# Trainium2 kernel of a hybrid SSD, attention and convolution block: the order of scan, gates and conformer tail, and the engine of the probability sums

## Chip, cores and metric

One core of one Trainium2 chip. The metric is the device time of one execution in microseconds, over several executions. The engines are TensorE (PE; its weight loads are PEld), VectorE (DVE), ScalarE (ACT) and GpSimd (POOL); SyncE (SP) issues all DMA transfers. All values are 32-bit floats.

## The reference, cut

Two layers over 1024 positions and a context of 256, width 1024. In each layer one projection gives ten parts, and three branches are joined again:

```python
z, xbc, dtr, q, k, v, ga, ua, ub, gc = split_cols(h @ w_in[i])
# SSD: silu of a depthwise convolution of 5 taps over xbc, then a scan both ways in chunks of 128
y_diag = einsum(C B^T, exp(cum_l - cum_s) masked, x dt)      # inside a chunk
y_off  = einsum(C, state that enters the chunk, exp(cum))
y = (y_f + y_b + d_skip * xs) * silu(z);  ssd = rmsnorm(y)
# attention: 12 heads over 4 key heads, 1280 keys
attn = attend(rope(rmsnorm(q)), [k, k_ctx], [v, v_ctx]) * silu(ga)
# conformer: convolution of 31 taps over ua * sigmoid(ub)
conv = (silu(layernorm(dwconv(u))) @ pw_w + pw_b) * silu(gc)
x = x + gate * (concat[ssd, attn, conv] @ w_out[i])
```

The context goes through the same blocks, in the last layer only as far as keys, values and states need it. SSD: 12 heads of 64, 2 groups, state 128, forward and backward.

## The kernel before, in words

All 1280 positions are ten tiles of 128 (in the second layer, the last, most work is for eight). Every projection matmul is three matmuls of rounded halves (`mm3`, L210: hh with wth, hl with wth, hh with wtl), in pieces of 512, 512 and 256 columns. A layer goes through these stages:

1. Norms and the k, v and q projections, position by position.
2. The feature-major blocks (`phase_b`, `block` L623). A block is two units of 128 features x 1280 positions; a unit is 72 matmuls. There are 17: nine of them alternate xbc (x, B and C of the SSD) with ub and ua of the conformer, then three blocks of z, two of gc, three of ga. What a unit of the first nine gives is convolved on DVE, xbc with 5 taps (xcv), u with 31 (cac, a chain of `scalar_tensor_tensor`). The unit of z, gc or ga is gated (`gate` L590) and stored to DRAM (gz_d, gc_d, ga_d).
3. `cm_tail` (L656), the rest of the conformer, stands beside the gc and ga blocks: transposes of cac, layernorm on DVE (statistics, a `pow` of one column on POOL, xn, lv), silu on ACT, the pointwise projection in groups of up to four tiles, gating by gc.
4. Attention (`attn` L904). A unit is two heads and two tiles of queries, 512 columns; 24 units see all keys, and in the first layer six more only the context's. `maxima` computes queries x keys and reduces over the keys' columns on DVE (a_sm), `scores` computes them again with the maxima subtracted through an extra row (q_b, k_b), ACT takes the exponential into a_p, `values` multiplies by vs. The denominators need a sum over the ten key tiles: a_p come in five pairs of 128 x 1024, of which four additions (a_ac, L974 and L978) make one; a last one of 512 (a_a, L981) feeds two matmuls. The list NG says, unit by unit, how many of these additions run on POOL; the others run on DVE.
5. `ssd` (L710), beside attention. For the nine backward states (chunk 9 to 1), then for the ten chunks in the order 8, 9, 0 to 7: POOL scales x (s_wx L732, s_xd L777) and decays the state (s_tm L735); cumulated decays are broadcast from DRAM to 128 partitions by DMA (s_cb, four of 384 KB a chunk), POOL subtracts a column (s_e L788), ACT takes relu and exp, POOL multiplies by C B^T (s_cm, L791). PE sums the output in 72 matmuls (s_e and s_xd, and s_yo through msk), DVE gates with z (s_yz), POOL scales and SP stores to ys_d. The term of the entering state is a matmul of hf or hb with s_cT, scaled on DVE (s_of L803) and added to s_yo on POOL (L806). The backward states stay in SBUF, one buffer each.
6. The output projection in two halves (`out_half` L1081), with the next layer's norms.

The order in which each engine runs its instructions is fixed when the program is built: a scheduler lays them on a modelled time line, where `at(t)` gives a piece of code its earliest time, and each engine then runs its own list strictly in sequence, waiting for data and for buffers. Constants such as SSD_PACE and TAIL are such times. Tiles come from pools with rings of buffers (`bufs`), so the next user of a ring waits for the last reader of the buffer. Pools are opened and closed as a stack, on the left or the right side of SBUF; a pool that is opened where another was waits for the closed one's last user.

## Time and profile before

| | |
|---|---|
| median of 3 runs | 2925.08 us (2920.04 to 2926.33) |
| profiled execution, its own time | 2926.13 us |
| its span | 2924.1 us, 41057 instructions |
| PE busy, mean granted clock | 2714.5 us (93%), 0.965 |
| DVE, POOL, ACT busy | 2175.7 (74%), 1165.6 (40%), 1062.2 (36%) |
| DMA | 314.44 MB, mean 108 GB/s |

PE's busy time is that of matmuls that overlap in its pipeline, so 93% is not 93% of its peak. The shares are means over stages with different limits; the prediction cuts the span into stages. A page of the profile names instructions by line, engine, operation, output and inputs; after a bar come busy time, mean ns of one, and the idle time of the engine ahead of them with what ended it.

### The profile page before, as it was taken

The numbers are of one execution on the slowest core, as the hardware profiler recorded it, in microseconds if no ns is written. First come the engines' busy times: TensorE is split into PE (matmuls) and PEld (weight loads), VectorE is DVE, ScalarE is ACT, GpSimd is POOL, SyncE is SP. The second block draws the span as 40 slices with busy tenths as digits, with TensorE's granted clock in tenths as the row PEclk, the third lists the DMA queues.
The fourth block names the chain that finished last, engine by engine and source line by source line (L and its number), as shares of the span: only waits on it lengthen the run. The fifth ranks groups of instructions, "written<-read, shape, count | busy, mean of one in ns | idle before, by whom it ended". The sixth has DMA issues, their size and how long they took to land. (4 is left out here: it accounts for less than half of the span.)

```text
span 2924.1 us, 41057 instructions
## 1 busy us (share of the span) xinstructions
PE 2714.5 (93%) x15708; PEld 2111.4 (72%) x15708; DVE 2175.7 (74%) x2987; ACT 1062.2 (36%) x1801; POOL 1165.6 (40%) x832
## 2 busy tenths in 40 slices
PE   5999998999998888999999999999998998999998
PEld 3888876888856655666787998877886665666676
DVE  4476899973299989797445587999835989898644
ACT  4212221222245454454335222222224454644432
POOL 2244122232168677571112352222323667675111
PEclk9999998999999989899999999999999999999999
...
GB/s 237 191 159 66 56 55 65 90 98 105 115 137 108 73 88 84 74 68 130 205 147 162 114 76 67 55 63 107 102 127 151 73 98 72 103 59 62 164 152 143
DMA packets 284035, 314.44 MB, mean 108 GB/s; under 512 B 27606, under 2 KB 219190, under 8 KB 282814
## 3 DMA queue, kind: packets, MB, share of 16 engines
...
q14 instruction: 74, 0.61, 0.1%
...
## 5 line engine op out<-in xcount | busy, mean ns | idle before, releaser
L193 PE MATMUL m<-hh,wth 128*128 128x512 f32 (+1 forms) x1440 | 533.7, 371 | 0.1
L193 PE MATMUL m<-hl,wth 128*128 128x512 f32 (+1 forms) x1440 | 532.2, 370 | 0.0
L193 PE MATMUL m<-hh,wtl 128*128 128x512 f32 (+1 forms) x1440 | 531.6, 369 | 0.0
L199 ACT ACTIVATE a_p<-m 128x512 f32<-128x512 f32 x492 | 285.5, 596 | 373.1 <-PE m L193 362.7
L208 DVE SCALAR_TENSOR_TENSOR cac<-up,cmw,cac 128x1295 f32<-128x1295 f32 (+1 forms) x240 | 383.2, 1617 | 1.9
L935 DVE TENSOR_REDUCE a_sm<-m 128x1 f32<-128x512 f32 (+1 forms) x600 | 331.0, 583 | 52.8 <-PE m L193 50.2
L359 POOL TENSOR_TENSOR wtl<-wr,wth 128x1024 fp32r<-128x1024 f32 x68 | 201.9, 2969 | 404.2 <-ACT wth L199 404.1
L193 PEld LDWEIGHTS m<-hh,wth 128*128 128x128 f32 x1440 | 273.0, 190 | 47.8 <-ACT th L199 0.5
L193 PEld LDWEIGHTS m<-hh,wtl 128*128 128x128 f32 x1440 | 272.5, 189 | 48.1
L193 PEld LDWEIGHTS m<-hl,wth 128*128 128x128 f32 x1440 | 272.7, 189 | 47.3
L193 PE MATMUL m<-q_a,k_a 128*128 128x512 f32 (+1 forms) x656 | 255.3, 399 | 23.1 <-ACT a_p L199 10.9
L193 PE MATMUL m<-k_a,q_a 128*128 128x512 f32 (+1 forms) x600 | 242.0, 440 | 24.9 <-DVE a_sm L935 19.3
L193 PE MATMUL t<-a_p,vs 128*64 128x256 f32 x1968 | 250.9, 397 | 0.9 <-ACT a_p L199 0.4
L193 PE MATMUL m<-woh,yl 128*128 128x512 f32 x576 | 227.7, 397 | 6.1 <-DVE yl L1101 5.9
L193 PE MATMUL m<-woh,yh 128*128 128x512 f32 x576 | 226.6, 396 | 5.2 <-ACT yh L199 5.2
L193 PE MATMUL m<-wol,yh 128*128 128x512 f32 x576 | 226.6, 395 | 0.8 <-DVE wol L1077 0.8
L193 PE MATMUL m<-q_b,k_b 65*128 65x512 f32 (+1 forms) x656 | 223.1, 350 | 0.0
L193 PEld LDWEIGHTS t<-a_p,vs 128*64 128x64 f32 x1968 | 138.7, 142 | 89.1 <-issue 17.2
L193 PEld LDWEIGHTS m<-q_a,k_a 128*128 128x128 f32 x656 | 129.3, 197 | 84.3 <-ACT a_p L199 23.4
L193 PEld LDWEIGHTS m<-k_a,q_a 128*128 128x128 f32 x600 | 117.0, 201 | 99.6 <-DVE a_sm L935 38.2
L199 ACT ACTIVATE wth<-wr 128x1024 fp32r<-128x1024 f32 (+1 forms) x84 | 89.3, 1063 | 255.6 <-DMA wr<-in_wfm 136.2
L193 PE MATMUL m<-wth,hh 128*128 128x256 f32 (+1 forms) x608 | 173.6, 288 | 1.3 <-ACT wth L199 0.8
...
## 6 DMA issues: line engine op xcount, KB each, us to landing
...
s_cb<-cum_d SPq DMA_DIRECT2D x72, 384.0 KB, 3.7
...
s_x<-xt_d SPq DMA_DIRECT2D x38, 384.0 KB, 3.2
yf<-ys_d SPq DMA_DIRECT2D x36, 384.0 KB, 3.9
yf<-ya_d SPq DMA_DIRECT2D x36, 384.0 KB, 4.2
...
```

The source lines that it names most:

```text
L193: P.matmul(o, l, r, start=start, stop=stop)
L199: S.activation(o, i, f, **k)
L208: V.scalar_tensor_tensor(o, i, s, i1, op0, op1)
L359: (e or G).tensor_tensor(lo[:, s], raw, hi[:, s].bitcast(F32), ALU.subtract)
L935: V.tensor_reduce(sm[:, 2 * x + t, j:j + 1], ps[:, 0:kn], axis=AX.X, op=ALU.max)
```

## The change

- The z blocks move in among the convolution blocks (the first twelve blocks are now x0 u0 x1 z0 u1 x2 u2 z1 x3 u3 x4 z2); two gc and three ga blocks follow.
- `ssd` is now called from `phase_b`, with its pool on the left stack, beside the last five blocks, with SSD_PACE 11.5. The attention's pools are opened after it is closed.
- In `ssd`, the broadcast lands in the s_e ring itself (four buffers, four tiles a chunk) and the s_cb ring is gone; for the backward direction the subtraction and relu become six activations of 128 columns with a bias on ACT; the multiplication by s_cm goes from POOL to DVE; backward states go through DRAM (hb_d) and a ring of two; s_tm shares a ring of two with s_of; PSUM tiles are spread over three pools.
- `cm_tail` moves beside attention, in groups of two tiles, 28 apart (TPACE); the convolved u goes through DRAM (cc_d, ct).
- NG = [4]: all four additions of 128 x 1024 run on POOL in every unit.

```diff
@@ -19,14 +19,15 @@
...
-TAIL = 40.0
-SSD_PACE = 25.0
+TAIL = 24.0
+TPACE = 28.0
+SSD_PACE = 11.5
...
-NG = [0, 1]
+NG = [4]
...
@@ -64,12 +65,12 @@
 
 
 TM_UNITS = [("k", 0), ("v", 0), ("q", 0), ("q", 1)]
-FM_UNITS = []
-for _j in range(5):
-    FM_UNITS.append((("xbc", 2 * _j), ("xbc", 2 * _j + 1)))
-    if _j < 4:
-        FM_UNITS.append((("ub", _j), ("ua", _j)))
-for _n, _c in (("z", 3), ("gc", 2), ("ga", 3)):
+_u = [[(("xbc", 2 * j), ("xbc", 2 * j + 1)) for j in range(5)], [(("ub", j), ("ua", j)) for j in range(4)],
+      [(("z", 2 * j), ("z", 2 * j + 1)) for j in range(3)]]
+FM_UNITS = [_u[k][j] for k, j in ((0, 0), (1, 0), (0, 1), (2, 0), (1, 1), (0, 2), (1, 2), (2, 1), (0, 3), (1, 3), (0, 4),
+                                  (2, 2))]
+NF = len(FM_UNITS)
+for _n, _c in (("gc", 2), ("ga", 3)):
     FM_UNITS += [((_n, 2 * j), (_n, 2 * j + 1)) for j in range(_c)]
 
 CO = {}
@@ -264,6 +265,8 @@
     ys_d = dr([6, 128, T], "ys_d")
     ya_d = dr([6, 128, T], "ya_d")
     yc_d = dr([4, 128, T], "yc_d")
+    hb_d = [dr([128, 768], f"hb_d{c}") for c in range(NT)]
+    cc_d = [dr([128, T], f"cc_d{j}") for j in range(4)]
...
@@ -553,6 +556,9 @@
             for k in range(1, 31):
                 at(t0 + k * pace)
                 stt(o[:, 0:NCM], u[:, k:k + NCM], cw[:, j, k:k + 1], o[:, 0:NCM], ALU.mult, ALU.add)
+            Y.dma_start(out=cc_d[j][:, 0:1024], in_=o[:, 0:1024])
+            if not last:
+                Y.dma_start(out=cc_d[j][:, 1024:1280], in_=o[:, 1039:1295])
 
...
@@ -642,69 +648,73 @@
                 if n == "xbc":
                     conv_x(j, tt)
 
-        for i in range(9):
+        for i in range(NF):
             block(i)
         s2.close()
 
 
+        g0 = b2 + NF * 26
         s3 = ExitStack()
-        tlp = pool(s3, f"tl{l}")
-        g0 = b2 + 9 * 26
-        for i in range(9, 14):
-            block(i)
-
-        def cm_tail(c0):
...
-        cm_tail(g0 + TAIL)
-        for i in range(14, 17):
+        sp = pool(s3, f"sp{l}")
+        ssd(l, sp, g0, sv)
+        for i in range(NF, len(FM_UNITS)):
             block(i)
         s3.close()
         st.close()
-        return g0 + 8 * 26, sv, st_r
+        return g0 + (len(FM_UNITS) - NF) * 26, st_r
+
+
+    def cm_tail(l, tlp, c0):
+        last = l == depth - 1
+        at(c0 - 10)
+        pwh, pwl = wblock(tlp, tlp, a["pww"][l], "pw", 1)
+        hc = mk(tlp, [128, 16], "hc")
+        ts(V, hc[:, 0:8], colc[l][:, CO["lng"][0]:CO["lng"][0] + 8], 0.5, ALU.mult)
+        groups = [(b, 2) for b in range(0, 8 if last else NT, 2)]
+        for tb, tn in groups:
+            uh = mk(tlp, [128, 4, 256], "uh", F32R)
+            ul = mk(tlp, [128, 4, 256], "ul", F32R)
+            for t in range(tb, tb + tn):
+                at(c0 + TPACE * t - 8)
+                ct = mk(tlp, [128, 4, 128], "ct", bufs=2)
+                for j in range(4):
+                    Y.dma_start(out=ct[:, j], in_=cc_d[j][:, 128 * t:128 * t + 128])
+                at(c0 + TPACE * t)
+                ps = mk(px, [128, 4, 128], "x")
+                for j in range(4):
+                    tr(ps[:, j, :], ct[:, j], idf)
+                bs = mk(tlp, [128, 12], "bs", bufs=2)
...
+                at(c0 + TPACE * t + 6)
+                ps2 = mk(px, [128, 4, 128], "x")
...
+            n = tn * 128
+            for f in range(4):
+                at(c0 + TPACE * (tb + tn - 1) + 14 + 3 * f)
+                gcs = mk(tlp, [128, 256], "gcs", bufs=2)
+                Y.dma_start(out=gcs[:, 0:n], in_=gc_d[f][:, tb * 128:tb * 128 + n])
+                ps = mk(px, [128, 512], "x")
...
+                Y.dma_start(out=yc_d[f][:, tb * 128:tb * 128 + n], in_=gcs[:, 0:n])
 
 
     def ssd(l, sp, c0, sv):
@@ -731,7 +741,7 @@
             wx = mk(sp, [128, 768], "s_wx", bufs=2)
             G.tensor_tensor(hv(wx), hv(xt), bc(wd[:, c, hs]), ALU.mult)
             if hin is not None:
-                tm = mk(sp, [128, 768], "s_tm", bufs=1)
+                tm = mk(sp, [128, 768], "s_of", bufs=2)
                 G.tensor_tensor(hv(tm), hv(hin), bc(et[:, c, hs]), ALU.mult)
             for g in range(2):
                 ps = mk(px, [128, 512], "x")
@@ -742,29 +752,35 @@
                 else:
                     V.tensor_copy(ho[:, s], ps[:, 0:384])
 
-        hb = {9: None}
+        hp = None
         t0 = c0 + 1
         for c in range(9, 0, -1):
             at(t0)
             t0 += 2
             xt, bt = load(c)
-            ho = mk(sp, [128, 768], f"hb{c - 1}")
-            state(c, 1, xt, bt, hb[c], ho)
-            hb[c - 1] = ho
+            ho = mk(sp, [128, 768], "hb", bufs=2)
+            state(c, 1, xt, bt, hp, ho)
+            if c <= 8 or not last:
+                Y.dma_start(out=hb_d[c - 1], in_=ho)
+            hp = ho
...
-                bT = mk(sp, [128, 2, 128], "s_bT", bufs=2)
+                bT = mk(sp, [128, 2, 128], "s_bT", bufs=1)
                 cT = mk(sp, [128, 2, 128], "s_cT", bufs=2)
                 tk = slice(128 * c, 128 * c + 128)
                 Y.dma_start(out=bT, in_=bT_d[:, :, tk].rearrange("g p t -> p g t"))
                 Y.dma_start(out=cT, in_=cT_d[:, :, tk].rearrange("g p t -> p g t"))
                 gz = mk(sp, [128, 6, 128], "s_gz", bufs=1)
                 Y.dma_start(out=gz, in_=gz_d[:, :, tk].rearrange("g p t -> p g t"))
-                ps = mk(px, [128, 512], "x")
+                hbc = None
+                if c != 9:
+                    hbc = mk(sp, [128, 768], "hb", bufs=2)
+                    Y.dma_start(out=hbc, in_=hb_d[c])
+                ps = mk(pt, [128, 512], "t")
                 for g in range(2):
                     mm(ps[:, 128 * g:128 * g + 128], bT[:, g, :], cT[:, g, :], True, True)
                 cm = mk(sp, [128, 2, 2, 128], "s_cm", bufs=1)
@@ -780,24 +796,27 @@
                 for g in range(2):
                     for d in range(2):
                         h0 = 12 * d + 6 * g
-                        cb = mk(sp, [128, 6, 128], "s_cb", bufs=2)
+                        e = mk(sp, [128, 6, 128], "s_e", bufs=4)
                         src = cum_d[24 * c + h0:24 * c + h0 + 6, :].rearrange("h t -> (h t)")
-                        Y.dma_start(out=cb.rearrange("p h t -> p (h t)"),
+                        Y.dma_start(out=e.rearrange("p h t -> p (h t)"),
                                     in_=src.unsqueeze(0).to_broadcast([128, 768]))
-                        e = mk(sp, [128, 6, 128], "s_e", bufs=4)
-                        G.tensor_tensor(e, cb, bc(cum[:, c, h0:h0 + 6], 6, 128), ALU.subtract)
-                        act(e, e, AF.Relu, scale=-1.0)
+                        if d:
+                            for j in range(6):
+                                act(e[:, j], e[:, j], AF.Relu, scale=-1.0, bias=cum[:, c, h0 + j:h0 + j + 1])
+                        else:
+                            G.tensor_tensor(e, e, bc(cum[:, c, h0:h0 + 6], 6, 128), ALU.subtract)
+                            act(e, e, AF.Relu, scale=-1.0)
                         act(e, e, AF.Exp, scale=-1.0)
-                        G.tensor_tensor(e, e, cm[:, d, g].unsqueeze(1).to_broadcast([128, 6, 128]), ALU.mult)
+                        V.tensor_tensor(e, e, cm[:, d, g].unsqueeze(1).to_broadcast([128, 6, 128]), ALU.mult)
                         E[d, g] = e
                 yo = mk(sp, [128, 768], "s_yo", bufs=1)
                 G.tensor_tensor(hv(yo), hv(xt), bc(rc(l, "d")), ALU.mult)
-                for d, hin in enumerate((hf, hb[c])):
+                for d, hin in enumerate((hf, hbc)):
                     if hin is None:
                         continue
-                    tm = mk(sp, [128, 768], "s_of", bufs=1)
+                    tm = mk(sp, [128, 768], "s_of", bufs=2)
                     for g in range(2):
-                        ps = mk(px, [128, 512], "x")
+                        ps = mk(pv_, [128, 512], "v")
                         mm(ps[:, 0:384], cT[:, g, :], hin[:, 384 * g:384 * g + 384], True, True)
...
@@ -1124,14 +1143,14 @@
         last = l == depth - 1
         st, sr, sw = ExitStack(), ExitStack(), ExitStack()
         pp = pool(st, f"pp{l}")
-        c0, sv, st_r = phase_b(l, nh, b0, pp)
+        c0, st_r = phase_b(l, nh, b0, pp)
         kp = pool(st, f"kp{l}")
         pre = attn_prep(l, kp, c0)
         st_r.close()
         nh[0].close()
         ap = pool(st, f"ap{l}")
-        sp = sr.enter_context(tc.tile_pool(name=f"sp{l}", bufs=1, side="right"))
-        ssd(l, sp, c0, sv)
+        tlp = sr.enter_context(tc.tile_pool(name=f"tl{l}", bufs=1, side="right"))
+        cm_tail(l, tlp, c0 + TAIL)
         sr.close()
```

What this does to the order of instructions is shown at three places. The first is PE in layer 0, where the gate matmuls end. Ahead of the change, from the middle of attention; m are scores (q_a, q_b against k_a, k_b) or keys' maxima (k_a first), and x one group of the SSD's output:

```order
L193 MATMUL m_8963<-q_a_8429,k_a_6708 128x512
L193 MATMUL m_8963<-q_b_8430,k_b_6709 128x512
L193 MATMUL m_8968<-k_a_8696,q_a_8759 128x512
L193 MATMUL m_8971<-k_a_8696,q_a_8759 128x512
L193 MATMUL m_8974<-q_a_8429,k_a_6708 128x512
L193 MATMUL m_8974<-q_b_8430,k_b_6709 128x512
L193 MATMUL x_7004<-msk_74,s_yo_6993 64x128 x2
L193 MATMUL x_7004<-s_e_6967,s_xd_966_6961 64x128 x2
L193 MATMUL x_7004<-s_e_6974,s_xd_967_6963 64x128 x2
```

Now, at the last gate matmul (m from wth, wtl and h), and on to the next chunk's output:

```order
L194 MATMUL m_7671<-hl_168,wth_7511 128x256
L194 MATMUL m_7671<-hh_167,wtl_7512 128x256
L194 MATMUL v_5649<-ones_78,s_s_772_5644 128x1
L194 MATMUL x_5663<-s_wx_5656,s_b_5541 128x384
L194 MATMUL v_5723<-hf_5655,s_cT_5671 128x384
L194 MATMUL x_5797<-s_wx_5793,s_b_5668 128x384
L194 MATMUL v_5726<-hf_5655,s_cT_5671 128x384
L194 MATMUL v_5731<-hb_5676,s_cT_5671 128x384
L194 MATMUL v_5734<-hb_5676,s_cT_5671 128x384
L194 MATMUL t_5739<-msk_74,s_yo_5720 64x128 x2
L194 MATMUL t_5739<-s_e_5688,s_xd_789_5684 64x128 x2
L194 MATMUL t_5739<-s_e_5694,s_xd_790_5686 64x128 x2
```

The output groups stood among the attention's matmuls; now PE's list has nothing but the scan between the last gate matmul and the next chunk's output, and so it goes on for eight chunks.

The second place is POOL in one chunk of the scan, layer 0. Before, from the norm's pow of one chunk to the last row ahead of the next chunk's subtractions (a_g and a_ac are the attention's):

```order
L833 TENSOR_TENSOR s_rs_7053<-s_rs_7053,neg_82 128x1
L794 TENSOR_TENSOR s_yo_7114<-s_x_7066,rowc_8_86 128x768
L1013 TENSOR_TENSOR a_g_8893<-a_g_8893,a_rc_9082 128x256
L732 TENSOR_TENSOR s_wx_7310<-s_x_7189,d_wd_1698 128x768
L735 TENSOR_TENSOR s_tm_7181<-hf_7057,d_et_1697 128x768
L1013 TENSOR_TENSOR a_g_9033<-a_g_9033,a_rc_9158 128x256
L974 TENSOR_TENSOR a_ac_1599_9107<-a_p_9114,a_p_9138 128x1024
L791 TENSOR_TENSOR s_e_7088<-s_e_7088,s_cm_7079 128x768
L791 TENSOR_TENSOR s_e_7102<-s_e_7102,s_cm_7079 128x768
L791 TENSOR_TENSOR s_e_7095<-s_e_7095,s_cm_7079 128x768
L791 TENSOR_TENSOR s_e_7109<-s_e_7109,s_cm_7079 128x768
L806 TENSOR_TENSOR s_yo_7114<-s_yo_7114,s_of_7116 128x768
```

Now, one chunk from its first subtraction on:

```order
L807 TENSOR_TENSOR s_e_5962<-s_e_5962,d_cum_1699 128x768
L793 TENSOR_TENSOR s_xd_857_5958<-s_x_5940,d_dt_1693 128x768
L793 TENSOR_TENSOR s_xd_858_5960<-s_x_5940,d_dt_1693 128x768
L846 TENSOR_TENSOR s_yo_5920<-s_yz_5875,colc_7_84 128x768
L745 TENSOR_TENSOR s_of_5932<-hf_5792,d_et_1711 128x768
L807 TENSOR_TENSOR s_e_5978<-s_e_5978,d_cum_1699 128x768
L852 TENSOR_TENSOR s_rs_5925<-s_rs_5925,neg_82 128x1
L813 TENSOR_TENSOR s_yo_5994<-s_x_5940,rowc_8_86 128x768
L742 TENSOR_TENSOR s_wx_6204<-s_x_6077,d_wd_1712 128x768
L825 TENSOR_TENSOR s_yo_5994<-s_yo_5994,s_of_5996 128x768
L825 TENSOR_TENSOR s_yo_5994<-s_yo_5994,s_of_6004 128x768
```

The multiplications by s_cm are gone from POOL, there are two subtractions instead of four, and the attention's instructions are gone from among them. The two additions of s_of come last, just ahead of the next chunk's first subtraction.

The third is DVE in attention, layer 0, around the sum of one unit's exponentials. Before:

```order
L935 TENSOR_REDUCE a_sm_9116<-m_9213 128x1
L974 TENSOR_TENSOR a_ac_1600_9108<-a_p_9176,a_p_9198 128x1024
L935 TENSOR_REDUCE a_sm_9116<-m_9223 128x1
L974 TENSOR_TENSOR a_ac_1600_9108<-a_ac_1600_9108,a_p_9221 128x1024
L937 TENSOR_REDUCE a_nm_9117<-a_sm_9116 128x4
L978 TENSOR_TENSOR a_ac_1600_9108<-a_ac_1599_9107,a_ac_1600_9108 128x1024
L935 TENSOR_REDUCE a_sm_9278<-m_9280 128x1
L981 TENSOR_TENSOR a_a_1634_9253<-a_ac_1600_9108 128x512
L935 TENSOR_REDUCE a_sm_9278<-m_9292 128x1
L820 TENSOR_TENSOR s_yz_7124<-x_7125,s_gz_7074 128x384
```

Now (bs, xn and lv are the conformer tail's):

```order
L687 BN_STATS bs_8281<-x_8276 128x6
L209 SCALAR_TENSOR_TENSOR lv_1276_8262<-lth_8261,lv_1276_8262 128x512
L954 TENSOR_REDUCE a_sm_9175<-m_9267 128x1
L688 BN_AGGR bs_8281<-bs_8281 128x2
L956 TENSOR_REDUCE a_nm_9176<-a_sm_9175 128x4
L206 TENSOR_SCALAR bs_8281<-bs_8281 128x1
L954 TENSOR_REDUCE a_sm_9315<-m_9317 128x1
L1000 TENSOR_TENSOR a_a_1565_9294<-a_ac_1530_9168 128x512
L206 TENSOR_SCALAR xn_8286<-x_8276,bs_8281 128x512
L954 TENSOR_REDUCE a_sm_9315<-m_9327 128x1
```

No a_ac is left on DVE; a_a reads what POOL has summed, and the tail's layernorm stands between the maxima, its xn behind a pow on POOL.

More of the change, by code (lines that the diff above doesn't have):

```diff
@@ L535, in phase_b @@
         b2 = b0 + 130
-        cmp_ = pool(st, f"cm{l}")
         s2 = ExitStack()
+        cmp_ = pool(s2, f"cm{l}")
         up_p = pool(s2, f"up{l}")
@@ L575, in conv_x @@
                 at(t0 + XLAG)
-                sg = mk(gp, [128, NT, 128], "xsg")
+                sg = mk(xp_p, [128, NT, 128], "xsg")
                 for ta in (0, 4, 8):
@@ L706, in phase_b @@
         st.close()
-        return g0 + 8 * 26, sv, st_r
+        return g0 + (len(FM_UNITS) - NF) * 26, st_r
[19 more added lines that the diff above has]
+                bs = mk(tlp, [128, 12], "bs", bufs=2)
+                V.bn_stats(bs[:, 0:6], ps.rearrange("p j t -> p (j t)"))
+                V.bn_aggr(bs[:, 6:8], bs[:, 0:6])
+                rs_pow(bs[:, 9:10], bs[:, 7:8], 1.0, bs[:, 8:9], 1)
+                xn = mk(tlp, [128, 512], "xn", bufs=1)
+                ts(V, xn, ps.rearrange("p j t -> p (j t)"), bs[:, 6:7], ALU.subtract, bs[:, 9:10], ALU.mult)
+                at(c0 + TPACE * t + 6)
+                ps2 = mk(px, [128, 4, 128], "x")
+                for j in range(4):
+                    tr(ps2[:, j, :], xn[:, 128 * j:128 * j + 128], idf)
+                th = mk(tlp, [128, 4, 128], "lth", bufs=1)
+                v2 = mk(tlp, [128, 4, 128], "lv2", bufs=1)
+                for j in range(4):
+                    g, b = hc[:, j:j + 1], hc[:, 4 + j:5 + j]
+                    ts(V, v2[:, j], ps2[:, j], g, ALU.mult, b, ALU.add)
+                act(th, v2, AF.Tanh)
+                stt(v2, th, 1.0, v2, ALU.add, ALU.mult)
+                o = (t - tb) * 128
+                act(uh[:, :, o:o + 128], v2, AF.Copy)
+                G.tensor_tensor(ul[:, :, o:o + 128], v2, uh[:, :, o:o + 128].bitcast(F32), ALU.subtract)
+            n = tn * 128
[4 more added lines that the diff above has]
+                ps = mk(px, [128, 512], "x")
+                pwx, ux = (pwh, pwl), (uh, ul)
+                mm3(ps[:, 0:n], lambda x, k: pwx[x][:, k, 128 * f:128 * f + 128],
+                    lambda x, k: ux[x][:, k, 0:n], 4)
+                stt(gcs[:, 0:n], ps[:, 0:n], cc(l, "pwb", f), gcs[:, 0:n], ALU.add, ALU.mult)
+                ts(V, gcs[:, 0:n], gcs[:, 0:n], 0.5, ALU.mult)
+                Y.dma_start(out=yc_d[f][:, tb * 128:tb * 128 + n], in_=gcs[:, 0:n])
@@ L808, in ssd @@
                 for g in range(2):
-                    ps = mk(px, [128, 512], "x")
+                    ps = mk(pt, [128, 512], "t")
                     for f3 in range(3):
@@ L821, in ssd @@
                                     gz[:, 3 * g:3 * g + 3, :], ALU.mult)
-                sq = mk(sp, [128, 6, 128], "s_of", bufs=1)
+                sq = mk(sp, [128, 6, 128], "s_of", bufs=2)
                 act(sq, yz, AF.Square)
```

47 lines of the change are left out of this document (1 added, 46 removed).

## The prediction

> **What bounds the kernel now.** I read the profiled execution first (span 2924.1 us, its own time 2926.13, 1.05 us over the median of the runs shown, so the sum needs no correction), then the table of windows, cut where the trace shows a stage's first or last instruction. Columns: window, length, then busy time (instructions) of PE, weight load, DVE, ACT, POOL, the granted clock, the DMA share, GB/s.
>
> ```profile
> 242.00:603.00 361.00, 336.45 (x1721) 284.10 (x1719) 332.27 (x228) 74.66 (x114) 85.95 (x65) 0.96 0.20 65
> 603.00:803.00 200.00, 195.78 (x1054) 166.56 (x1054) 76.42 (x158) 49.11 (x81) 44.96 (x31) 0.99 0.32 108
> 803.00:1364.00 561.00, 501.46 (x3292) 339.40 (x3292) 494.53 (x693) 286.94 (x493) 369.37 (x221) 0.93 0.30 92
> 2228.00:2736.00 508.00, 465.09 (x3019) 313.91 (x3018) 451.15 (x635) 260.20 (x446) 314.25 (x187) 0.95 0.29 89
> ```
>
> These are, for layer 0, the convolution blocks and first z gates (up to the last conformer tap), the other gates with the conformer tail, then attention with the SSD scan beside it; the fourth row is layer 1's attention. Gates run at PE's pace, 195.78 of 200 us. The convolution stage is bound twice, PE 336 and DVE 332 of 361. In attention DVE binds: 494.53 of 561 is 88%, and 451.15 of 508 is 89%. POOL, 369, is next. So attention is where a gain must come from, and DVE is what must be relieved. Of DVE's groups in layer 0 (a window that begins 13 us earlier; after the bar stand busy time and mean ns) these are the ones that go:
>
> ```profile
> L974 DVE TENSOR_TENSOR a_ac<-a_ac,a_p 128x1024 f32<-128x1024 f32 x34 | 59.2, 1743 | 1.8 <-ACT a_p L199 1.6
> L974 DVE TENSOR_TENSOR a_ac<-a_p,a_p 128x1024 f32<-128x1024 f32 x24 | 34.3, 1427 | 2.1 <-ACT a_p L199 2.0
> ...
> L978 DVE TENSOR_TENSOR a_ac<-a_ac,a_ac 128x1024 f32<-128x1024 f32 x12 | 25.9, 2157 | 0.5
> L978 DVE TENSOR_TENSOR a_ac<-a_p,a_ac 128x1024 f32<-128x1024 f32 x11 | 20.5, 1867 | 0.2
> L803 DVE TENSOR_TENSOR s_of<-x,d_ec 128x384 f32<-128x384 f32 x36 | 19.4, 540 | 1.8 <-PE x L193 1.7
> L825 DVE TENSOR_REDUCE s_s<-s_of 128x128 f32<-128x768 f32 x10 | 15.2, 1518 | 1.9 <-ACT s_of L199 1.9
> ```
>
> The four a_ac groups, sums of exponentials over the keys, are 59.2 + 34.3 + 25.9 + 20.5 = 139.9 us. The SSD's own groups are 19.4 and 15.2 here, and with the smaller ones (gating, state copies, masks, scalars) about 75.
>
> **The change, part by part.**
>
> *Probability adds.* All 1024-wide adds go to POOL. DVE loses 139.9 us in layer 0. POOL has four adds per unit where it had half of one; the row for its price:
>
> ```profile
> L974 POOL TENSOR_TENSOR a_ac<-a_p,a_p 128x1024 f32<-128x1024 f32 x12 | 29.8, 2484 | 4.2 <-ACT a_p L199 4.2
> ```
>
> 24 full units times 4 times 2.48 are 238 us on POOL. It can afford that only because the SSD leaves attention: of today's 369 the output's scaling keeps about 24, and 24 + 238 + some 23 of tail is near 285.
>
> *Conformer tail beside attention.* Its prices, from where it runs now, among the gates:
>
> ```profile
> L205 DVE TENSOR_SCALAR lv<-x,hc 128x128 f32<-128x128 f32 x40 | 13.6, 402 | 11.7 <-POOL ul L689 7.9 <-PE x L196 3.8
> L208 DVE SCALAR_TENSOR_TENSOR lv<-lth,lv 128x512 f32<-128x512 f32 x10 | 11.1, 1109 | 1.1 <-ACT lth L199 0.9
> L205 DVE TENSOR_SCALAR xn<-t,bs 128x512 f32<-128x512 f32 x10 | 8.1, 805 | 4.4 <-PE x L196 4.2
> L672 DVE BATCH_NORM_STATS2 bs<-t 128x6 f32<-128x512 f32 x10 | 6.9, 690 | 1.7 <-PE t L196 1.7
> L208 DVE SCALAR_TENSOR_TENSOR gcs<-v,colc,gcs 128x256 f32<-128x256 f32 x4 | 1.9, 484 | 12.8 <-PE v L193 12.8
> L203 DVE TENSOR_SCALAR gcs<-gcs 128x256 f32<-128x256 f32 x4 | 1.2, 294 | 0.1
> ```
>
> A tile costs DVE 4 x 0.40 + 1.1 + 0.8 + 0.7 + 0.3 (small) and half of four feature blocks' 0.48 + 0.29, 6.1 us; ten tiles are 61, eight 49. New DMA stores and loads of the convolution (cc_d, ct) are 64 KB each on SP; I cost them at nothing, since the gates' windows show a DMA share near 0.3, and if ct came late a tile's first transposes would hold PE for one landing, some 3 us.
>
> *What attention can then take.* DVE in layer 0: 494.5 - 139.9 - 75 + 61 = 340 us. PE's floor I count at its dense pace, from rows where nothing waits:
>
> ```profile
> 787.77 0.40 PE L193 MATMUL m<-hh,wtl 128*128 128x512 f32 x1
> 788.00 0.39 PE L193 MATMUL m<-hh,wth 128*128 128x512 f32 x1
> ...
> L193 PE MATMUL t<-a_p,vs 128*64 128x256 f32 x976 | 126.1, 398 | 0.3
> L193 PE MATMUL m<-k_a,q_a 128*128 128x512 f32 x192 | 85.6, 485 | 6.3 <-DVE a_sm L935 3.3 <-ACT q_a L199 1.7 <-ACT a_p L199 0.9
> L193 PE MATMUL m<-q_a,k_a 128*128 128x512 f32 x168 | 78.5, 467 | 6.7 <-ACT a_p L199 3.3 <-DVE a_sm L935 2.9
> ```
>
> Starts are 0.234 us apart for 512 columns, so half of that, 0.117, for 256. Per layer 0: 528 matmuls of 512 columns (192 + two lists of 168), 456 of 256, 976 + 112 of 256 on the probabilities, some 320 transposes of 0.065: 325 us; the tail adds 33, of which 7 run before attention. So 351, and PE becomes the bound, DVE just behind it. Layer 1 by its share of PE busy time (465.09 to 501.46, 0.927): 325. I take the fill that the binding engine reaches there now, 88%: 399 and 369 us, where 561 and 508 stand. Saved: 162 + 139 = 301. Bounds: 83% (two engines near equal, one waiting on the other in order) gives 815 in all and saves 254; 95%, nearly the gates' fill, gives 712 and saves 357.
>
> *SSD ahead of attention.* The order shows that beside the last five gate blocks PE has the nine backward states and, in layer 0 alone, two of ten output chunks; eight chunks stand behind the last gate matmul in both layers, with no other PE work, and the attention's pool opens when theirs closes. So these eight are exposed. Gates' end first. One gate unit (ACT's copies of the same kind of piece, one unit apart):
>
> ```profile
> 767.90 0.38 ACT L199 ACTIVATE g_t<-m 128x256 f32<-128x256 f32 x1 [2.24 <-PE m L193]
> 781.90 0.38 ACT L199 ACTIVATE g_t<-m 128x256 f32<-128x256 f32 x1 [2.24 <-PE m L193]
> ...
> 795.99 0.28 PE L193 MATMUL m<-hh,wtl 128*128 128x256 f32 x1
> 803.33 1.22 PE L193 MATMUL m<-k_a,q_a 128*128 128x512 f32 x2 [0.99 <-ACT q_a L199]
> ...
> 2217.08 0.39 PE L193 MATMUL m<-hh,wtl 128*128 128x512 f32 x1
> ```
>
> A unit is 14.0 us, and total gate work is unchanged. PE loses the tail, 96 x 0.234 + 48 x 0.117 + 80 transposes at twice a 128-column matmul's 0.055 (an estimate) = 37 us, gains nine state pairs and two chunks, 18, and should lose some 8 of the 25 us that it idles in the first two windows, since z blocks fill in. Layer 0: 796.3 - 37 + 18 - 8, about 768. Layer 1, with eight tiles and no chunk: 2217.3 - 30 + 10 - 6, about 2192.
>
> *Period of one exposed chunk.* Rows of POOL, PE, ACT and the DMA:
>
> ```profile
> 1000.23 1.48 POOL L732 TENSOR_TENSOR s_wx<-s_x,d_wd 128x768 f32<-128x768 f32 x1 [4.92 <-PE x L193]
> 1012.52 1.84 POOL L806 TENSOR_TENSOR s_yo<-s_yo,s_of 128x768 f32<-128x768 f32 x1
> L833 POOL TENSOR_TENSOR s_rs<-s_rs,neg 128x1 f32<-128x1 f32 x10 | 5.4, 541 | 9.0 <-DVE s_rs L205 9.0
> 891.46 0.44 PE L193 MATMUL x<-msk,s_yo 128*64 128x128 f32 x4
> 891.73 0.61 PE L193 MATMUL x<-s_e,s_xd 128*64 128x128 f32 x8
> ...
> L199 ACT ACTIVATE n_h<-x,msh,msc 128x128 f32<-128x128 f32 x40 | 15.0, 459 | 5.4 <-PE x L196 4.4 <-POOL hl L346 0.7 <-DVE msc L208 0.2
> L199 ACT ACTIVATE s_e<-s_e 128x768 f32<-128x768 f32 x80 | 66.2, 840 | 22.8 <-POOL s_e L788 21.8
> ...
> s_cb<-cum_d SPq DMA_DIRECT2D x72, 384.0 KB, 3.7
> ys_d<-s_yo SPq DMA_DIRECT2D x18, 384.0 KB, 2.7
> ```
>
> POOL's program order in one chunk is e-subtract, two xd, the gating of the chunk before, the state decay, e-subtract, pow, yo, wx (2 x 1.47 + 2 x 1.48 + 1.47 + 1.47 + 0.54 + 2 x 1.48 = 12.3 us), then two yo additions of 1.84 that wait for DVE's s_of behind PE's state and inter-chunk matmuls. PE gives these only after wx, in order, through a PSUM ring that DVE empties (0.54 each): 2 us more. So yo is whole at 12.3 + 2 + 3.7 = 18 us. Only then can the output matmuls of the first group start, 36 of 0.055, 2.0 us; they free the two e buffers into which the next broadcast lands, 3.7 us after its issue. Sum 23.7; I take 23.5. ACT, six 128-wide relus of 0.46 in place of one of 0.84 for two of four tiles, comes to 2 x 1.7 + 2 x 3.6 = 10.6, and runs beside POOL; DVE's part, with four e multiplications new to it, too. Bounds: 21.5 (additions at 1.48, no wait for s_of), 26 (PE at half pace throughout). Nothing of the period is POOL's old e multiplication, which does go.
>
> The next two rows are the same pair of state matmuls, where PE had stood and where it was busy:
>
> ```profile
> 2226.14 1.65 PE L193 MATMUL x<-s_wx,s_b 128*128 128x384 f32 x2 [0.96 <-POOL s_wx L732]
> ...
> 1100.20 0.81 PE L193 MATMUL x<-s_wx,s_b 128*128 128x384 f32 x2
> ```
>
> 0.81 us against 1.65: after a stall PE runs at half pace. In the exposed chunks it would be busy for a fifth of the time, so up to 2 us of each period hang on this; they are within the bounds. The Trainium skill, "TensorE: Matmul & The Clock Gate", section "What's actually happening", states that after an idle window of about 3.4 us the array clock is halved. The pair of rows agrees. By that rule the first group takes 4.0 us, the period is 25.5, and the sum below rises by 15 x 2 = 30 us.
>
> After the last chunk: gating and the store of ys_d (2.7 us) hold the pool's release, then the loads of k (as s_cb, 3.7), then the preparation, which in layer 1 takes some 10 us from the last gate matmul at 2217 to the first state pair and maxima at 2226 and later: 20 us together, where 7 and 10 us now follow the gates.
>
> **Sum.** First maxima in layer 0: 768 + 8 x 23.5 + 20 = 976, 173 us after today's 803.3. Layer 1: 2192 + 4 + 7 x 23.5 + 20 = 2380.5, 152.5 after 2228. Together +325. Attention: -301. Projections and output halves: the same instructions, nothing. 2926 + 24 = **2950 us**. Each us of period is worth 15 us and each per cent of fill 8.6, so these two settle the sign.
>
> **Rivals.**
>
> *Attention packs denser than any DVE-bound stage of today, and the kernel is faster.* With no SSD between them, PE and ACT alternate in large pieces; ACT now spends this on PE:
>
> ```profile
> ACT a_p L199 <- PE m L193: 186.8, 119, 7.2
> PE t L193 <- DVE a_a L981: 28.2, 17, 5.9
> ```
>
> For it: the convolution stage fills two engines to 92% and 93% at once. Against it: the last row's wait for the denominators, which after the change come from POOL's fourth addition. At 93% and a period of 22: +161 + 142 - 342 = -39, 2887 us. The point from which it decides is a fill of 676 / 744 = 91% at my period, or a period of 21.9 at my fill. Chance 0.38.
>
> *POOL's queue holds DVE.* The tail's 128x1 pow stands on POOL among additions of 2.4 us, and DVE's normalisation waits for it with the maxima queued behind, on which PE's PSUM waits. One to two additions for each of 18 tiles, 44 to 88 us, less what PE's buffers cover; the fill falls to 83 or 84%, and with a period of 25: +185 + 163 - 264 = +84, 3010 us. For it: DVE and POOL orders, strictly in sequence. Chance 0.17.
>
> *The change does what its words say*, the scan hidden beside the gates. Its order speaks against it; with a period of POOL's bare 16 us all would shrink by 15 x 7.5 = 112, to 2838. Chance 0.03, within the faster case.
>
> The Trainium skill, "GPSIMD Engine Reference", section "4.1 Engine selection", prefers VectorE for elementwise additions, at half of GpSimd's time; POOL's 2.48 against DVE's 1.43 above agrees in direction. With the additions left on DVE, as that rule would have it, DVE's 340 would be 480 and attention at 88% 545, so that I hold the rule not to bear here as long as POOL is under the bound.
>
> **How the numbers follow.** 0.2% (5.9 us) is about what a measurement of this kernel can tell from no change: faster is under 2919, slower over 2931. My forecast, slower by some 6 to 60 us, has 0.36; the POOL rival 0.17; the faster rival 0.38; between them, gain and loss within 5.9 us, 0.09. Slower is thus 0.53. As both signs hold much, the forecast's own range is 2932 to 2985. The range, 2865 to 3010, goes from a fill of 95% with a period of 21.5 (+157 + 138 - 357 = -62) to the POOL rival, and leaves out 0.1 at each end.
>
> **What would show it.** First maxima near 976 and 2380, last gate matmul near 768 and 2192; eight groups of 72 output matmuls 23 to 24 us apart with a granted clock far below 0.9 there; DVE free of a_ac, POOL near 285 us in layer 0's attention; attention of 399 and 369 us with PE about 88% full at its dense pace. I am wrong if chunks follow each other at 20 us or less, if attention is under 375 and 350, or if the gates end before 755.

## The result, and the profile after

The changed kernel takes **3211.39 us** (median of 4 runs, 3209.05 to 3215.3) against 2925.35 before: ratio 1.0983, 95% interval 1.0964 to 1.1002, **286 us slower**. The forecast had the direction (slower), but 2950 us, outside its range of 2865 to 3010.

Windows of the changed kernel, cut as those of before (busy us of PE, PEld, DVE, ACT, POOL; granted clock; DMA share; GB/s): the scan alone, the preparation and attention of layer 0, then the same of layer 1.

```profile
784.00:1022.00 238.00, 125.50 (x716) 80.73 (x718) 108.03 (x148) 75.59 (x157) 145.72 (x91) 0.67 0.39 118
1022.00:1049.00 27.00, 16.66 (x102) 13.82 (x98) 10.78 (x27) 10.56 (x19) 3.83 (x4) 0.75 0.54 159
1049.00:1534.00 485.00, 448.10 (x2739) 311.05 (x2739) 339.28 (x595) 241.68 (x440) 267.49 (x142) 0.94 0.18 53
2352.00:2584.00 232.00, 124.48 (x737) 78.39 (x735) 97.47 (x145) 67.21 (x138) 138.46 (x86) 0.71 0.41 122
2584.00:2610.00 26.00, 17.11 (x83) 14.65 (x82) 10.35 (x27) 10.79 (x19) 3.83 (x4) 0.65 0.58 165
2610.00:3036.00 426.00, 401.54 (x2481) 277.22 (x2482) 307.04 (x512) 218.76 (x397) 258.19 (x132) 0.96 0.17 50
```

In 784 to 1022 no engine is near full: POOL is busy for 146 of 238 us (61%) and PE for 125 (53%), at a granted clock of 0.67. In layer 0's attention DVE is busy for 339 of 485 us (the forecast's 340) and POOL for 267 (forecast 285); PE is at 448, 92% by its records, which overlap. The marks of this table are each read off the first or last row of its kind in the trace (attention from the first a_sm to the last a_g, so that it ends 21 and 8 us later than the windows of before did):

| us | before | forecast | after |
|---|---|---|---|
| layer 0: gates' end | 796 | 768 | 784 |
| first maxima | 804 | 976 | 1050 |
| attention | 581 | -162 | 481 (-100) |
| attention's end to layer 1's gates' end | 832 | -25 | 821 |
| gates' end to first maxima | 11 | 188 | 260 |
| attention | 516 | -139 | 422 (-93) |
| rest | 180 | 180 | 177 |

246 - 100 - 11 + 248 - 93 - 3 = 287, before rounding. The time ahead of attention costs 494 us, attention returns 193, and 14 come from the rest.

One chunk of the scan, from its first subtraction to the next chunk's (a choice of the timeline's rows: start, duration, engine, line, operation, and in brackets the idle time before it with its releaser):

```profile
876.47 1.47 POOL L807 TENSOR_TENSOR s_e<-s_e,d_cum 128x768 f32<-128x768 f32 x1 [8.08 <-DMA s_e<-cum_d]
...
882.20 2.27 DVE L810 TENSOR_TENSOR s_e<-s_e,s_cm 128x768 f32<-128x768 f32 x1
...
882.33 0.59 PE L194 MATMUL v<-ones,s_s 128*128 128x1 f32 x2 [7.63 <-DVE s_s L844]
...
884.46 2.15 DVE L810 TENSOR_TENSOR s_e<-s_e,s_cm 128x768 f32<-128x768 f32 x1
...
886.54 0.55 DVE L751 TENSOR_TENSOR hf<-x,s_of 128x384 f32<-128x384 f32 x1
...
887.14 1.65 PE L194 MATMUL x<-s_wx,s_b 128*128 128x384 f32 x2 [4.21 <-DVE hf L751]
...
889.24 1.47 POOL L742 TENSOR_TENSOR s_wx<-s_x,d_wd 128x768 f32<-128x768 f32 x1
889.30 2.22 DVE L810 TENSOR_TENSOR s_e<-s_e,s_cm 128x768 f32<-128x768 f32 x1
...
891.44 0.54 DVE L822 TENSOR_TENSOR s_of<-v,d_ec 128x384 f32<-128x384 f32 x1
...
893.69 1.81 POOL L825 TENSOR_TENSOR s_yo<-s_yo,s_of 128x768 f32<-128x768 f32 x1 [2.99 <-DVE s_of L822]
...
896.12 0.56 DVE L822 TENSOR_TENSOR s_of<-v,d_ec 128x384 f32<-128x384 f32 x1 [1.00 <-PE v L194]
...
896.82 1.80 POOL L825 TENSOR_TENSOR s_yo<-s_yo,s_of 128x768 f32<-128x768 f32 x1 [1.32 <-DVE s_of L822]
...
898.67 0.62 PE L194 MATMUL t<-msk,s_yo 128*64 128x128 f32 x4 [2.59 <-POOL s_yo L825]
...
902.32 2.79 SPq L801 DMA_DIRECT2D s_e<-cum_d  x4
...
906.13 1.47 POOL L807 TENSOR_TENSOR s_e<-s_e,d_cum 128x768 f32<-128x768 f32 x1 [7.51 <-DMA s_e<-cum_d]
```

29.7 us. DVE adds the forward state at 886.5, behind two multiplications of e in its queue, though POOL's decay was done at 883.7. PE's state and inter-chunk matmuls follow at half pace (1.65 us for one, which the trace shows as two records). The first s_of stands behind another multiplication of e, at 891.4; then three more matmuls and s_of take turns in one PSUM buffer, until 896.7. POOL has ended wx at 890.7 and waits 3.0 us for s_of; in 13 of the 16 exposed chunks it waits for s_of ahead of its first addition, 0.8 to 5.1 us. So the chain runs through the queues of ACT, which is at relu and exponentials until 882.2, and DVE, and not through POOL's. yo is whole at 898.6; the first output group takes 3.7 us; the broadcast lands 3.8 us after its issue at 902.3. The eight chunks of layer 0 follow each other every 27.6 to 31.0 us (mean 29.6), those of layer 1 every 25.9 to 32.7 (mean 29.1).

In layer 1's attention the starts of a_nm (once per unit) tell three kinds of units: six beside the tail, whose last store is issued at 2762.4 (first to second row: 19.5 us each); three beside the splitting of the output projection's weights on DVE (second to third row: 19.1 us each); and eight later ones (fourth to last row: 14.3 us each):

```profile
2647.17 0.14 DVE L956 TENSOR_REDUCE a_nm<-a_sm 128x4 fp32r<-128x12 f32 x1
...
2763.95 0.17 DVE L956 TENSOR_REDUCE a_nm<-a_sm 128x4 fp32r<-128x12 f32 x1
...
2821.13 0.17 DVE L956 TENSOR_REDUCE a_nm<-a_sm 128x4 fp32r<-128x12 f32 x1
...
2882.22 0.17 DVE L956 TENSOR_REDUCE a_nm<-a_sm 128x4 fp32r<-128x12 f32 x1
...
2996.91 0.17 DVE L956 TENSOR_REDUCE a_nm<-a_sm 128x4 fp32r<-128x12 f32 x1
```

### The profile page after: what moved, and what is told of

It is laid out like the page before. It is cut to its first block, busy times and chain, and to the rows that moved or that the text cites. A ratio compares the mean times of both kernels' runs of the same rounds, so it can differ in the third digit from the quotient of the medians.

```text
span 3210.9 us, 42166 instructions
## 1 busy us (share of the span) xinstructions
PE 2814.5 (88%) x15900; PEld 2175.6 (68%) x15900; DVE 2023.7 (63%) x2923; ACT 1101.6 (34%) x1981; POOL 1327.9 (41%) x892
## 5 line engine op out<-in xcount | busy, mean ns | idle before, releaser
L209 DVE SCALAR_TENSOR_TENSOR cac<-up,cmw,cac 128x1295 f32<-128x1295 f32 (+1 forms) x240 | 405.1, 1693 | 3.9
L993 POOL TENSOR_TENSOR a_ac<-a_ac,a_p 128x1024 f32<-128x1024 f32 x144 | 346.2, 2404 | 66.7 <-ACT a_p L200 60.3
L194 PE MATMUL m<-q_a,k_a 128*128 128x512 f32 (+1 forms) x656 | 242.0, 379 | 23.3 <-DVE a_sm L954 14.0
L194 PE MATMUL m<-k_a,q_a 128*128 128x512 f32 (+1 forms) x600 | 225.1, 417 | 24.6 <-DVE a_sm L954 17.1
L194 PE MATMUL t<-a_p,vs 128*64 128x256 f32 x1968 | 241.1, 391 | 0.7 <-ACT a_p L200 0.3
```

Of the source, the lines that this page charges most:

```text
L194: P.matmul(o, l, r, start=start, stop=stop)
L209: V.scalar_tensor_tensor(o, i, s, i1, op0, op1)
L993: e.tensor_tensor(o, prev[-1], pt2, ALU.add)
```

## The experiments

The theory after reading this: (1) the scan alone is a chain, and its price is its exposed length; (2) the tail among the units is what keeps attention from the full gain; (3) the additions' engine matters little. Rivals: the static order of gates and attention is worse in itself, or POOL's additions set the unit. All but the last are single runs with a profile, beside runs of before on the same chip (2925 to 2929 us). Eleven runs of before on one chip spread over 11 us (2920.86 to 2932.28), so a single run that differs by less says nothing.

**Without the tail, and with the additions back on DVE.**

```diff
# e1_no_tail: cm_tail reduced to gcs <- gc_d, yc_d <- gcs
# e2_ng01
-NG = [4]
+NG = [0, 1]
```

> The changed kernel without the conformer tail's arithmetic (the pointwise branch is left out: gc is copied to yc_d). In the changed kernel's layer 1 the units of attention follow each other every 14.2 us once the tail has ended, and every 18.5 us beside it. Theory A, the tail among the in-order queues is what stretches those units: all units come near 14 us, layer 1's attention falls from 426 us to 365-380, layer 0's by 45-65, the total by 90-130. Theory B, POOL's four additions in series set the unit, with or without the tail: only the tail's own 33 us of PE work per layer can go, units beside it stay over 17 us, the total falls by less than 50.

> The changed kernel with the additions back on DVE as before (none or one of four on POOL). Theory A: DVE takes 3.5 x 1.6 us more per unit, 10.8 to 16.4, so the units after the tail go from 14.2 to 17 or more, attention grows by 50-80 us per layer, the total by 100-160. Theory B, DVE and PE wait for POOL's chain of additions: attention shrinks by 20-60 us in all.

e1: 3138.36 us. e2: 3209.68 us. Attention of layers 0 and 1 in e1, then in e2 (windows):

```profile
1055.00:1486.00 431.00, 405.76 (x2477) 273.70 (x2476) 279.88 (x473) 219.55 (x401) 250.24 (x126) 0.96 0.11 34
2583.00:2960.00 377.00, 366.90 (x2286) 249.11 (x2285) 252.23 (x418) 200.20 (x364) 244.54 (x120) 0.98 0.11 32
```

```profile
1046.00:1525.00 479.00, 442.71 (x2726) 304.24 (x2726) 413.11 (x673) 239.55 (x436) 69.77 (x58) 0.95 0.18 53
2608.00:3027.00 419.00, 394.38 (x2456) 271.57 (x2456) 373.64 (x589) 217.60 (x393) 58.86 (x47) 0.96 0.17 50
```

e1's attention is 431 and 377 us, 50 and 46 shorter; PE is 97% busy in the second, and most units of layer 1 are near 14 us. That is theory A, but the total fell by 73, less than the expected 90, since here the time from the gates' end to the first maxima is 13 us longer in layer 1 and 5 in layer 0. In e2 DVE does 74 us more in layer 0 and POOL 198 less, and the time stays (3209.68 against 3211.39), though DVE is now busy for 413 of 479 us, 86%. Both theories missed there: A had expected 100 to 160 us more, B 20 to 60 less. In this kernel's attention the engine of the additions makes no difference that a run can tell.

**Without the scan, in both kernels.**

```diff
# e5_after_no_scan, e6_before_no_scan: in ssd(), for each chunk only
+yg <- gz_d; ys_d <- yg; rss = 1
```

> The changed kernel without the scan (left out: all of it; z's gate is copied to ys_d). Theory, the scan stands alone on the path between the gates and attention in the changed kernel, 247-266 us per layer with its preparation: first maxima come 10 us after the gates' end, attention stays 480 and 422 us, the total is 2690-2730. Rival, the gates or attention would stretch anyway (their static order is what is bad): total over 2800.

> The kernel before without the scan (left out in the same way). Theory, beside attention the scan costs only its share of the binding VectorE, 75 and 66 us, and some waits: attention 460-490 and 420-450 us, the total 2760-2800, so the scan's price is about 150 us there and about 500 in the changed kernel. Rival, it was nearly free (under 60 us in all) or already half exposed (over 250).

e5: 2700.71 us. e6: 2674.71 us. Attention in e5, then in e6:

```profile
770.00:1262.00 492.00, 456.29 (x2803) 317.32 (x2802) 359.33 (x620) 243.45 (x443) 273.78 (x147) 0.94 0.20 58
2076.00:2523.00 447.00, 411.34 (x2542) 286.87 (x2541) 324.69 (x534) 220.49 (x399) 263.12 (x136) 0.95 0.18 52
```

```profile
807.00:1261.00 454.00, 419.24 (x2480) 275.57 (x2480) 376.08 (x577) 230.50 (x422) 54.21 (x43) 0.94 0.20 59
2103.00:2491.00 388.00, 371.83 (x2274) 246.50 (x2274) 339.12 (x517) 209.26 (x380) 47.19 (x36) 0.96 0.19 54
```

The scan's price is 3211 - 2701 = 511 us in the changed kernel, and the rival "over 2800" is out: the static order of the rest is not what is bad. In the kernel before it is 2929 - 2675 = 254, not the theory's 150: the rival's "over 250", more than a share of DVE. The difference of 257 us is nine tenths of the change's 286. Most of what is left shows between e5 and e6, which differ by 26 us and have no scan: the gates of e5 end 41 us earlier in layer 0 (758, 799) and, counted from the attention's end, 29 earlier in layer 1; attention is 39 us longer in layer 0 and 59 in layer 1 (489 and 445 against 451 and 386 from first maxima to last a_g), where the tail now runs. So attention loses 98 us where the gates gain 70: the rest of the change, the tail's move above all, does not pay. (In the changed kernel attention took 481 and 422 us, so that it did not stay as it was in e5.)

**The chain of a chunk.** Four edits to the changed kernel:

```diff
# e3_vring: entering state's matmuls in the gates' ring; e7_vx: in two buffers
-ps = mk(pv_, [128, 512], "v")
+ps = mk(pm, [128, 512], "m")                       # e3
+ps = mk(*((px, ..., "x") if g else (pv_, ..., "v")))  # e7
# e4_ering
-e = mk(sp, [128, 6, 128], "s_e", bufs=4)
+e = mk(sp, [128, 6, 128], "s_e", bufs=6)           # gz in s_yz's tile, s2 in bT's
# e9_one_load: e <- cb1 - cum, cb1 loaded once per layer; gz in s_yz's tile
```

> The changed kernel, where the matmuls of the entering state write to the ring of four PSUM buffers (m) and not to the single buffer (v). One exposed chunk takes 29.7 us in the changed kernel; four rounds of matmul and DVE scaling take turns in one buffer there, 1.56 us each. Theory: this series is on the path, the period falls by 3 to 4 us and the total by 45-60. Rival, the path runs through POOL's order and the broadcast, and the series is hidden: under 15 us.

> The changed kernel, where the matmuls of the entering state take turns in two PSUM buffers (v and x), so that PE's next one need not wait for VectorE's scaling, and the gates' ring is left alone. Theory, this series is on the chain of a chunk: period 29.7 to 26.5-28, total 25-50 lower. Rival, the chain goes another way: within 10 us of 3211.

> The changed kernel with six s_e buffers instead of four (to make room, z's gate is loaded into the tile of s_yz, and the squares' sums go to the tile of s_bT), so that the next chunk's first two broadcasts land ahead. Theory: the 3.6 us of the first output group and the 3.8 us of the broadcast's landing, which stand between two chunks now, leave the path: period 22-24 us, total 85-125 lower. Rival, POOL's additions and PE's order hold the next chunk anyway: period above 28, total less than 30 lower.

> The changed kernel with one broadcast of decays per layer in place of four per chunk (left out: the decays of all other chunks and heads, so the scan's numbers are not the reference's; the work on every engine stays). The s_e buffers are still waited for, the landing is not. Theory: the 3.8 us between the issue after the first output group and the first subtraction are on every chunk's chain: period 29.7 to 25-26.5, total 45-75 lower. Rival, POOL and PE fill the time with other steps of the chain: period over 28.5, total less than 20 lower.

e3: 3286.61 us, 75 slower, though its chunks follow each other every 26 us: nine of layer 0's ten chunks now stand ahead of the last gates (gates and scan share a ring there, which is the likely reason), and PE's clock is 0.74 there (windows of e3, the scan and then the gates):

```profile
700.00:910.00 210.00, 107.89 (x789) 77.30 (x788) 100.83 (x134) 71.92 (x152) 137.25 (x86) 0.74 0.44 133
910.00:1070.00 160.00, 150.78 (x807) 125.84 (x806) 30.88 (x48) 31.24 (x55) 31.89 (x17) 0.97 0.20 70
```

e7 leaves the gates' ring alone: 3181.31 us, 30 lower, and four chunks in 102.2 us, 25.6 each (first s_yz of a chunk):

```profile
858.91 0.56 DVE L839 TENSOR_TENSOR s_yz<-t,s_gz 128x384 f32<-128x384 f32 x1 [4.26 <-PE t L194]
...
961.11 0.56 DVE L839 TENSOR_TENSOR s_yz<-t,s_gz 128x384 f32<-128x384 f32 x1 [4.40 <-PE t L194]
```

All of layer 0's exposed chunks come 25.7 us apart and those of layer 1 26.7. So some 4 us of the period in layer 0, and 2.4 in layer 1, were the one buffer. The total fell by less, because layer 0's attention is 16 us longer in e7; the runs do not say why. e4: 3244.19 us, 33 slower, period 31. It did not bring what it was meant to: SP still issues the four loads of a chunk in one run, at the end of the first output group, so the run says nothing on the landing. e9: 3190.38 us, 21 lower, three chunks in 81.6 us, 27.2 each, between its theory's 25 to 26.5 and its rival's 28.5:

```profile
866.76 0.56 DVE L839 TENSOR_TENSOR s_yz<-t,s_yz 128x384 f32<-128x384 f32 x1 [5.86 <-PE t L194]
...
948.38 0.56 DVE L839 TENSOR_TENSOR s_yz<-t,s_yz 128x384 f32<-128x384 f32 x1 [5.72 <-PE t L194]
```

Without the landing a chunk is 2.4 us shorter in layer 0, not the whole 3.8: POOL then waits 3.5 us for the output group that frees s_e, and 0.8 for PE's last reads of s_xd. As in e4, z's gate shares the tile of s_yz here, so the landing may be worth somewhat more or less than these 2.4.

**PE's half pace.**

```diff
# e8_warm: 48 fillers a chunk, e10_warm2: 18; one of three and of five places:
+for _ in range(n): mm(ps[:, 256:512], idf, xt[:, 0:256], True, True)
```

> The changed kernel with 48 idle matmuls added to each chunk (x times the identity into PSUM regions that are not read or are overwritten), which fill PE's waits. PE now runs at half pace there: the first output group takes 3.6 us where 36 matmuls take 2.0 beside attention. Theory, the half pace lengthens a period by 3-5 us: the clock rises from 0.67 to over 0.85 in the window, the period falls to 25-27.5, the total by 35-70. Rival, PE's pace is hidden behind POOL's waits, or the fillers delay as much as they gain: within 15 us, or slower.

> The changed kernel with 18 idle matmuls of 256 columns per chunk (8 after the C B^T products, 2 or 4 behind each scaling of the entering state), each placed in a wait of PE. Theory, half pace costs the chain 2-4 us of a period: the first output group falls from 3.6 towards 2.0 us, the period to 26.5-28.5, the total by 20-50. Rival: within 10 us of 3211 or slower, and the first group stays at 3.6 us or more.

e8: 3495.55 us, the rival's outcome, and no test of the pace, because the fillers alone take longer than PE's waits: two of a chunk's three runs of them took 8.4 and 10.5 us. Timeline of e8:

```profile
911.62 8.36 PE L195 MATMUL t<-s_x,msk 128*128 128x256 f32 x36
...
928.42 10.48 PE L195 MATMUL v<-s_yz,msk 128*128 128x384 f32 x32
```

e10: 3217.33 us. The clock of its scan windows is 0.87 (0.67 in the changed kernel). Timeline of e10, the first row of a chunk's first output group and the first of its second:

```profile
902.83 0.44 PE L194 MATMUL t<-msk,s_yo 128*64 128x128 f32 x4
...
904.85 0.39 PE L194 MATMUL t<-msk,s_yo 128*64 128x128 f32 x4
```

The group takes 2.0 us where it took 3.7 (898.67 to 902.36 in the changed kernel). But each pair of fillers but the first, which takes 2.0, stands 1.1 us in the series of the entering state, and the period is 30.2 in layer 0 and 28.9 in layer 1, as without fillers (29.6 and 29.1). The pace itself is shown (1.7 us of the group); what it costs the whole chain is not, since every filler that warms PE also delays it.

**A version from one part of the change.** Relu and subtraction of the backward direction on ACT and one or two additions on POOL, in the kernel before; then ACT for both directions with two additions, and a second scan buffer in PSUM:

```diff
# b1_relu_ng12 on before.py
-NG = [0, 1]
+NG = [1, 2]
+if d: for j in range(6): act(e[:, j], cb[:, j], AF.Relu, scale=-1.0, bias=cum[:, c, h0 + j:h0 + j + 1])
# b3_relu_all_ng2: for both d, NG = [2];   b4_px2: b1 with PM = 3, PX_ = 2
```

> The kernel before, with one part of the change (subtract and relu of the backward direction on ScalarE, six activations) and what that frees on POOL spent on additions: one or two of four on POOL (NG = [1, 2]). VectorE binds attention at 88%: it loses 24 x 1.6 = 38 us per layer, POOL 369 - 33 + 58. Theory: 20-30 us per layer, total 2865-2890. Rival, with POOL near 400 of 530 its in-order queue holds the others: within 10 us of 2925.

> The same with both directions on ScalarE (POOL loses 66 us, ScalarE gains 76) and two of four additions on POOL in every unit: VectorE loses 36 x 1.6 = 58 us per layer. Theory: 30-45 us per layer, total 2835-2870. Rival: ScalarE's twelve small activations per pair delay the exponentials on which PE waits; within 10 us of 2925 or slower.

> The kernel before with ScalarE's relu and one or two additions on POOL (2913 us in its run), and two PSUM buffers for the scan (x) against three for the scores (m). In the kernel before all of a chunk's products, states and outputs take turns in one buffer, and a chunk takes 49 us beside attention. Theory, that ring paces the scan and the scan paces attention: chunks every 35-42 us, total 2850-2890. Rival, the scores need their fourth buffer more: over 2913.

> The same kernel as b1_relu_ng12, to see whether its 0.4 to 0.5% is real. Theory: ratio to the kernel before 0.994 to 0.997. Rival: 1.000 within 0.002.

b1: 2913.05 us, b3: 2917.34, b4: 3091.08. b1 and b3 brought far less than their theories' 2865 to 2890 and 2835 to 2870. b4's chunks came faster (43 us for 49 in layer 0), but its gates ended 25 us later and its attention was 65 and 39 us longer than before's: the rival, though the ring that lost a buffer serves the gates as well as the scores. b1 again, 6 runs: 2912.28 us, **ratio 0.9947, interval 0.9931 to 0.9963**: half a per cent faster than the kernel before, and so faster than both. Its attention windows:

```profile
803.00:1364.00 561.00, 505.18 (x3345) 344.08 (x3346) 468.29 (x681) 309.72 (x600) 381.12 (x228) 0.92 0.32 95
2228.00:2736.00 508.00, 472.08 (x3078) 321.72 (x3077) 428.01 (x619) 281.00 (x536) 340.48 (x197) 0.96 0.31 92
```

DVE lost 26 and 23 us there. Attention, from first maxima to last a_g, is 555 us in layer 0 and 500 in layer 1, 25 and 16 shorter than before, but layer 1's gates end only 4 us earlier (2213 against 2217): 21 of layer 0's 25 us are lost again. The traces show where, first before, then b1:

```profile
1337.35 0.37 SPq L828 DMA_DIRECT2D ys_d<-s_yo  x1
...
1343.30 0.80 SPq L1090 DMA_DIRECT2D gt<-gt_d  x2
...
1364.24 0.47 PE L193 MATMUL m<-woh,yh 128*128 128x512 f32 x1
```

```profile
1336.79 0.37 SPq L832 DMA_DIRECT2D ys_d<-s_yo  x1
...
1341.45 0.80 SPq L1094 DMA_DIRECT2D gt<-gt_d  x2
...
1354.65 1.12 PE L193 MATMUL t<-a_a,twos 128*64 128x256 f32 x4 [3.26 <-DVE a_a L985]
...
1358.60 1.19 PE L193 MATMUL m<-woh,yh 128*128 128x512 f32 x2 [2.83 <-issue]
```

Waits of SP's queue in the same stretch, before and b1 (us in total, times, longest):

```profile
SPq L1090 <- DVE rss L203: 5.5, 1, 5.5
```

```profile
SPq L1094 <- DVE rss L203: 4.2, 1, 4.2
```

The first load of the output projection (gt) waits in both for the scan's last row on DVE (rss); the loads of its weights and inputs follow in SP's queue. The scan's last store is issued at the same time in both kernels, 1337, so the output projection starts at 1359 and not at 1364, while attention's last matmul falls from 1381 to 1355. Layer 0's chunks still come every 48 us or so. So the load on DVE was a bound only in part: in layer 0 the end of the scan's chain beside attention sets when the next stage can start. A kernel with that chain alone made shorter was not run.

## Why the prediction was wrong

Right: the order's reading (eight chunks alone in each layer), DVE's 340 us in attention, POOL's load there (285 forecast, 267 measured), and the sign for the reason given, exposed chunks against a shorter attention. But the sign hung on 325 - 301, and had a chance of 0.53. Of the 261 us between 2950 and 3211 (the three terms come to some 268; the rest of the program gives a few back):

- **The period of an exposed chunk, the term of 23.5 us, was 29.6** in layer 0 and 29.1 in layer 1: some 90 us of the miss. The step that failed is the overlap: ACT's and DVE's part, "with four e multiplications new to it", was to run beside POOL's order, and the entering state was to cost "2 us more" behind wx. In the chunk shown DVE's multiplications hold back the forward state and the first s_of, the four turns end 6.0 us after wx, and from the end of wx to the whole yo it takes 7.9 us and not 5.7. POOL's own order to the end of wx took 14.2 us and not 12.3, though POOL then waits; the first group 3.7 and not 2.0, the landing 3.8 as forecast; together 29.7 for 23.7. Of this the single buffer can give back some 4 us (e7). The bound of 26 had not summed these; the half pace was in the text as a thing within the bounds and should have been a term: PE, which was to be busy for a fifth of the time, is busy for 53% of it.
- **What stands around the eight chunks.** The first chunk's output came 26 us after layer 1's gates and not 4, from the last period's end to the first maxima it took 30 us in each layer and not 20, and the gates ended 16 and 14 us later than I had them: some 70 us together. The stores, reloads and preparation also ran at a clock of 0.65 to 0.75.
- **Attention, -301 forecast, -193 measured: 108 us.** The failed step is one fill, 88%, for all units and for the whole stage. By the prediction's own count of PE's floor (0.117 us for 256 columns) the eight late units of layer 1 reach 87%, which bears it out for units alone; the six beside the tail reach 77%, the three beside the weights' splitting 69%. (The 97% of e1 is PE's busy share, whose records overlap.) The tail was added as work, 26 and 24 us of PE; it costs 50 and 46 (e1), some 40 us more, both layers together, than that work at 88%. The other 70 or so stand in e1 too, which has no tail; the runs do not split them.
- **DVE as what must be relieved.** With the scan gone from attention PE is the fullest engine, as the sum said; but then the additions' move, which the text credits with 139.9 us of DVE time, is worth nothing (e2). The gain of attention is the scan's absence alone: in e6, with the additions left as they were, attention is 130 us shorter in each layer.

The rival of POOL's queue named the wrong wait. DVE waited 3 us in all for the pow; it did wait for POOL's fourth addition, but e2, without most of that wait, takes as long (waits of the changed kernel in layer 0's attention: us in total, times, longest):

```profile
DVE a_a L1000 <- POOL a_ac L993: 32.6, 13, 5.9
...
DVE xn L206 <- POOL bs L274: 3.0, 3, 1.3
```

The faster rival, a denser attention, did not come: even the late units stay at 87%. The rule of the Trainium skill, "GPSIMD Engine Reference", section "4.1 Engine selection", which prefers VectorE for elementwise additions, made no difference here either way (e2: 3209.68 us with the additions on DVE, 3211.39 with them on POOL).

The pair of rows behind the clock's half pace shows the halving (0.81 and 1.65 us), but the slow one stands after a wait of 0.96 us, not of 3.4. In the changed kernel longer waits do stand ahead of slow rows: 7.6 us at 882.33 and 4.2 at 887.14. The clock rule of the Trainium skill, "TensorE: Matmul & The Clock Gate", section "What's actually happening", moved the sum the right way, by 30 us, about a tenth of what was missing.
